# Where ScalarE's convolution products lie: raw weight buffers or scratch buffers

## The chip, the cores and the metric

The kernel runs on one core of a Trainium2 chip. The metric is the device time of one execution in microseconds (us), the median over runs. The engines are named as in the profile: PE is TensorE (matmuls, with PEld its weight loads), DVE is VectorE, ACT is ScalarE, POOL is GpSimd and SP is SyncE, whose queue issues the loads of the weights.

## The reference

It is a network of three blocks on 256 tokens of width 1024, all in float32: a first block (attention, a gated delta rule and a feed-forward net), then two layers of a second network, the first ("even") with a state-space scan and a convolution side by side, the second ("odd") with a gated recurrence; each of the two ends with a mixture of experts. The change is in the convolution of the even layer, a depthwise convolution of 31 taps over 1024 channels, done for 256 context tokens and, row by row of 64, for the 256 latent tokens:

```python
def dwconv(x, w, b):
    k = w.shape[0]
    y = lax.conv_general_dilated(x, w[:, None, :].astype(x.dtype), window_strides=(1,),
                                 padding=[(k // 2, k // 2)], dimension_numbers=("NWC", "WIO", "NWC"),
                                 feature_group_count=x.shape[-1])
    return y + b.astype(y.dtype)

def conformer_conv(v, gate, dw_w, dw_b, ln_g, ln_b, rows):
    u = v * jax.nn.sigmoid(gate)
    b, n, ch = u.shape
    if rows is not None:
        u = u.reshape(b * rows, GRID_W, ch)
    u = dwconv(u, dw_w, dw_b).reshape(b, n, ch)
    return jax.nn.silu(layernorm(u, ln_g, ln_b))
```

`v` and `gate` are columns of a projection of the tokens by the weight `ab_w_in` (1024 wide input).

## The kernel before, in words

Matmuls are made with each float32 operand split into a high and a low part, so that one product is three matmuls (L313 to L315: high by high, low by high, high by low). A weight comes through `load_split` (L277): SyncE loads a piece of 128x1024 floats into a buffer of tag `raw` (L284), ScalarE casts it to the high part `wh` (L287), and VectorE, or GpSimd for every third piece, subtracts to make the low part `wl` (L292). There are six `raw` buffers and three each of `wh` and `wl`. A buffer of a tag is handed to the next tile of that tag when its last reader is done. The order of instructions on each engine, and which buffer a tile gets, are settled by a scheduler before the program runs; on the chip each engine follows its queue.

The projection for the convolution is made in channel blocks of 128, two at a time (`proj_fm`, L317): for each pair first the gates (`g_cons`, L1108: a sigmoid on ScalarE into `cfg`), then the values (`v_cons`, L1119). One such projection of two blocks takes two pieces of the weight, for input rows 0 to 511 and 512 to 1023; both blocks use both pieces. After these eight projections come the state-space inputs (`bc_block`, `xs_block`, with their own convolution of 5 taps, `conv5`, L1206), again two pieces for two blocks.

The eight channel blocks of the long convolution are done in three ways:

- blocks 0, 2 and 4 on VectorE: 30 taps of two spans each, one multiply-add a span (L1165), into the accumulator `cf`;
- blocks 1 and 3 on GpSimd: ScalarE multiplies the whole input `us` by one tap (L1151) into half of a product tile `cfp`, and GpSimd adds its two spans to the accumulator (L1153). Two products share a tile of 128x1024 floats. This is 30 products, 15 tiles and 60 additions a block;
- blocks 5, 6 and 7 on TensorE: the input goes into a padded tile `up` (cleared by GpSimd at L1128, written by VectorE at L1130 and L1132), DMAs of SyncE spread it into `cr` (L1174), and 64 matmuls against diagonal weights `dg` make the sums (L1190).

The work of the first two kinds is not issued where it is written. `conv_v` yields small steps, which lie in a list for VectorE and one for ScalarE; `tick` (L989) takes some of them after other instructions: two from ScalarE's list after each cast of a weight piece, three from VectorE's after each subtraction, five after a product `us`. With `issue_after` a step is queued behind that instruction on its engine:

```python
TICKS = {"w": 3, "u": 5, "c5": 2, "E": 2, "z": 3, "aw": 2, "aE": 1}
CONV_POOL = (1, 3)
CONV_PE = (5, 6, 7)

ins = nc.scalar.activation(hi, raw, AF.Copy)
self.tick(ins, "aw", "a")
```

The scratch tag `t4` has three buffers of 1024 floats (`POOLS = dict(raw=6, raw2=2, wh=3, act=13, tmp=5, t4=3, ps=(3, 2, 2, 1))`, `t4` at L220). In this layer it holds the squares for the norms (`sq`), the scan's sums `ac2` (L1055, from here to the last of the masks of the scan, L1297), the three padded inputs `up`, half of the masks `E` (L1290) and later the centred tokens `cft`.

Of the kernel before, what the change touches and what calls it, by code (L numbers as in the profile page):

```python
# [7 lines left out]
F32 = mybir.dt.float32  # L8
# [10 lines left out]
P = 128  # L19
# [891 lines left out]
class Net(Net1):  # L911
# [99 lines left out]
    def even_mixer(self):  # L1011
# [123 lines left out]
        def conv_v(b, g):  # L1135

            acc = cf[b // 4][:, b % 4, :]
            w = lambda j: C("cf_dw_w_2", b * 32 + j)
            rows = lambda t: t[:, 256:].rearrange("p (r w) -> p r w", r=4)
            pool = b in CONV_POOL  # L1140
            if pool:
                yield lambda: nc.scalar.activation(acc, g, AF.Identity, scale=w(15), bias=C("cf_dw_b_2", b))
            else:
                yield lambda: nc.vector.tensor_scalar(acc, g, w(15), C("cf_dw_b_2", b), op0=ALU.mult, op1=ALU.add)
            pr = None

            def product(j, n):
                nonlocal pr
                if n % 2 == 0:
                    pr = self.wp.tile([P, 2, 512], F32, tag="raw", name="cfp", bufs=self.nraw)  # L1150
                nc.scalar.activation(pr[:, n % 2], g, AF.Copy, scale=w(j))  # L1151
                for a, s in spans(j, pr[:, n % 2]):
                    nc.gpsimd.tensor_tensor(a, a, s, ALU.add)  # L1153

            def spans(j, g):
                d = j - 15
                lo, hi = max(0, -d), max(0, d)
                return ((acc[:, lo:256 - hi], g[:, lo + d:256 - hi + d]),
                        (rows(acc)[:, :, lo:64 - hi], rows(g)[:, :, lo + d:64 - hi + d]))
            for n, j in enumerate([*range(15), *range(16, 31)]):  # L1160
                if pool:
                    yield lambda n=n, j=j: product(j, n)
                    continue
                for a, s in spans(j, g):
                    yield lambda a=a, s=s, j=j: nc.vector.scalar_tensor_tensor(a, s, w(j), a, op0=ALU.mult, op1=ALU.add)  # L1165
# [1416 lines left out]
```

## Time and profile before

| what | value |
|---|---|
| time, median of 3 runs | 2175.76 us (2174.41 to 2177.12) |
| profiled execution, its own time | 2166.01 us |
| its span, first to last instruction | 2163.9 us |
| mean granted clock of TensorE | 0.971 |
| busy share of the span: PE, DVE, ACT, POOL | 92%, 52%, 39%, 30% |
| products `cfp` (ACT, L1151) | 60, from 753.8 to 966.7 us |
| raw weight loads of `ab_w_in` (SP, L284) | 40, from 681.3 to 978.3 us |

All times of instructions are from the start of the span of that one profiled execution. Idle time of an engine stands in square brackets in a timeline, with what ended it.

### The profile page before, as it was taken

To read this page: it belongs to the slowest core of one execution; us is meant where nothing else is said; L and a number is where in the kernel's file an instruction comes from. 1 tells how busy PE (TensorE), PEld (TensorE's weight loads), DVE (VectorE), ACT (ScalarE), POOL (GpSimd) and SP (SyncE) were. 2 spreads that over 40 slices of the span, in tenths; PEclk is the share of its full clock that TensorE was granted. 3 is DMA by queue.
4 is the path that set the end of the run, shared out by engine and by line. 5 is a ranking of instruction groups with operands and counts; after the bars stand their busy time and mean duration, and the time that the engine had idled before them with its cause. 6 is when DMAs were issued, how large, how long until landed. Compare 5 with 4: busy or idle time off the path is not lost. (4 is left out here: it accounts for less than half of the span.)

```text
span 2163.9 us, 30084 instructions
## 1 busy us (share of the span) xinstructions
PE 2000.4 (92%) x11456; PEld 1451.1 (67%) x11456; DVE 1116.7 (52%) x1992; ACT 853.6 (39%) x1394; POOL 648.8 (30%) x515
## 2 busy tenths in 40 slices
PE   7999999989998889988889999998999999899996
PEld 6899877779976666766768746663487666634342
DVE  5755553554435754877686623331625556633332
ACT  5553455454334444654444132320335555411111
POOL 1413322224332255556655122121312223101110
PEclk9999999999999999989999999999999999999998
DMA  7534556667775126221124799998645224999993
GB/s 236 154 108 138 156 182 200 214 194 239 225 241 161 30 68 158 69 68 59 31 91 143 255 365 350 356 368 325 229 136 186 89 96 154 327 343 396 395 335 137
DMA packets 282844, 433.12 MB, mean 200 GB/s; under 512 B 33722, under 2 KB 159290, under 8 KB 282432
## 3 DMA queue, kind: packets, MB, share of 16 engines
q1 hardware_dynamic: 261696, 407.17, 56.0%
q10 hardware_dynamic: 16528, 10.12, 1.7%
q0 software_dynamic: 4464, 13.79, 1.7%
q8 instruction: 93, 1.52, 0.3%
q14 instruction: 63, 0.52, 0.1%
HBM read 420.17 MB, written 9.54 MB: 199 GB/s over the span
## 5 line engine op out<-in xcount | busy, mean ns | idle before, releaser
L287 ACT ACTIVATE wh<-raw 128x1024 fp32r<-128x1024 f32 x288 | 303.1, 1057 | 374.7 <-PE mm L314 146.3
L292 DVE TENSOR_TENSOR wl<-raw,wh 128x1024 fp32r<-128x1024 f32 x196 | 260.6, 1332 | 296.4 <-ACT wh L287 293.5
L292 POOL TENSOR_TENSOR wl<-raw,wh 128x1024 fp32r<-128x1024 f32 x92 | 222.0, 2413 | 578.8 <-ACT wh L287 539.6
L2054 PE MATMUL mm<-we,xs 128*64 128x512 f32 x832 | 195.6, 614 | 13.2 <-DVEq L2215 9.0
L2054 PEld LDWEIGHTS mm<-we,xs 128*64 128x64 f32 x832 | 61.7, 141 | 135.9 <-issue 117.7
L1165 DVE SCALAR_TENSOR_TENSOR cf<-us,cols,cf 128x200 f32<-128x200 f32 (+14 forms) x180 | 121.9, 724 | 0.1
L2070 DVE TENSOR_TENSOR hh<-mm,hh 128x512 f32<-128x512 f32 x19 | 13.1, 692 | 204.2 <-PE mm L2054 136.8
L1153 POOL TENSOR_TENSOR cf<-cf,cfp 128x241 f32<-128x241 f32 (+14 forms) x120 | 93.7, 811 | 70.9 <-ACT cfp L1151 70.9
L2069 ACT ACTIVATE hh<-mm 128x512 f32<-128x512 f32 x22 | 13.1, 598 | 223.9 <-PE mm L2054 162.4
L313 PE MATMUL mm<-fh,wh 128*128 128x256 f32 x352 | 101.1, 287 | 0.0
L315 PE MATMUL mm<-fh,wl 128*128 128x256 f32 x352 | 100.0, 284 | 0.9 <-POOL wl L292 0.9
L314 PE MATMUL mm<-fl,wh 128*128 128x256 f32 x352 | 99.7, 283 | 0.0
L313 PE MATMUL mm<-uh,wh 128*128 128x256 f32 x320 | 96.6, 302 | 0.0
L315 PE MATMUL mm<-uh,wl 128*128 128x256 f32 x320 | 91.8, 287 | 1.8 <-DVE wl L292 1.5
L314 PE MATMUL mm<-ul,wh 128*128 128x256 f32 x320 | 92.9, 290 | 0.0
L2040 POOL TENSOR_TENSOR h<-h,yz 128x512 f32<-128x512 f32 x16 | 25.0, 1565 | 221.9 <-DVE yz L2039 221.9
L315 PE MATMUL mm<-ev0h,wl 128*128 128x512 f32 (+1 forms) x168 | 66.6, 397 | 8.4 <-DVE wl L292 8.4
L313 PEld LDWEIGHTS mm<-fh,wh 128*128 128x128 f32 x352 | 67.5, 192 | 5.4 <-issue 5.4
L313 PE MATMUL mm<-ev0h,wh 128*128 128x512 f32 (+1 forms) x168 | 68.0, 406 | 0.7 <-ACT wh L287 0.7
L315 PEld LDWEIGHTS mm<-fh,wl 128*128 128x128 f32 x352 | 67.5, 192 | 1.4 <-POOL wl L292 1.3
L313 PE MATMUL mm<-ev1h,wh 128*128 128x512 f32 (+1 forms) x168 | 65.8, 392 | 2.5 <-ACT wh L287 2.5
L2054 PE MATMUL mm<-we,hT 128*64 128x512 f32 x208 | 60.9, 600 | 7.5 <-ACT hT L1934 7.5
(968 smaller groups left out, 5228.8 us busy)
## 6 DMA issues: line engine op xcount, KB each, us to landing
mraw<-in_mod_w SPq DMA_DIRECT2D x96, 512.0 KB
we<-in_moe_w_gate SPq DMA_DIRECT2D x37, 1024.0 KB
raw<-in_w_in SPq DMA_DIRECT2D x72, 512.0 KB
we<-in_moe_w_down SPq DMA_DIRECT2D x35, 1024.0 KB
we<-in_moe_w_up SPq DMA_DIRECT2D x32, 1024.0 KB
we<-in_moe_w_up SPq DMA_DIRECT2D x52, 512.0 KB
we<-in_moe_w_down SPq DMA_DIRECT2D x46, 512.0 KB
we<-in_moe_w_gate SPq DMA_DIRECT2D x42, 512.0 KB
```

The costliest lines, as they stand in the source:

```text
L287: ins = nc.scalar.activation(hi, raw, AF.Copy)
L292: ins = eng.tensor_tensor(lo, raw, hi.bitcast(F32), ALU.subtract)
L313: mm(out, lh, rh, start=start, stop=False)
L314: mm(out, lh, rl, start=False, stop=False)
L315: return mm(out, ll, rh, start=False, stop=stop)
L1153: nc.gpsimd.tensor_tensor(a, a, s, ALU.add)
L1165: yield lambda a=a, s=s, j=j: nc.vector.scalar_tensor_tensor(a, s, w(j), a, op0=ALU.mult, op1=ALU.add)
L2040: (nc.gpsimd if d else nc.vector).tensor_tensor(x[:, t, ds], x[:, t, ds], z, ALU.add)
L2054: nc.tensor.matmul(out[r], x[0][:, k, r], w, start=start, stop=stop)
L2069: nc.scalar.activation(hh, pg[2 * i], AF.Silu)
L2070: nc.vector.tensor_tensor(hh, pg[2 * i + 1], hh, ALU.mult)
```

## The change

Product tiles take a buffer of tag `t4` in place of one of tag `raw`. Shape, size and type of the tile are the same (two halves of 512 floats), and all instructions stay.

```diff
@@ -1147,7 +1147,7 @@
             def product(j, n):
                 nonlocal pr
                 if n % 2 == 0:
-                    pr = self.wp.tile([P, 2, 512], F32, tag="raw", name="cfp", bufs=self.nraw)
+                    pr = self.t4([P, 2, 512], name="cfp")
                 nc.scalar.activation(pr[:, n % 2], g, AF.Copy, scale=w(j))
                 for a, s in spans(j, pr[:, n % 2]):
                     nc.gpsimd.tensor_tensor(a, a, s, ALU.add)
```

```python
def t4(self, shape=None, dt=F32, name="t4"):
    return self.tp.tile(shape or [P, 1024], dt, tag="t4", name=name, bufs=self.n4)
```

## Rows read from the trace of the kernel before

**Rows 1.** The page, busy us, share of the span and instructions of each engine

```profile
PE 2000.4 (92%) x11456; PEld 1451.1 (67%) x11456; DVE 1116.7 (52%) x1992; ACT 853.6 (39%) x1394; POOL 648.8 (30%) x515
```

**Rows 2.** Instructions on tile `cfp`: ns min/median/max, first and last start

```profile
L1151 ACT ACTIVATE cfp<-us,cols x60: 701/710/754, 753.8 to 966.7; 128x512 f32<-128x512 f32 x60
```

**Rows 3.** Windows: stretch, length, busy us (instructions) PE, PEld, DVE, ACT, POOL, clock, DMA

```profile
750.00:860.00 110.00, 98.06 (x629) 75.01 (x632) 62.64 (x86) 48.93 (x68) 62.22 (x71) 0.97 0.41 108
```

**Rows 4.** Timeline of PE: start, us, what, count, idle time before and its releaser

```profile
763.84 0.50 PE L313 MATMUL mm<-ev0h,wh 128*128 128x512 f32 x1 [0.70 <-ACT wh L287]
...
784.48 0.80 PE L315 MATMUL mm<-ev0h,wl 128*128 128x512 f32 x1 [8.10 <-DVE wl L292]
...
823.65 0.51 PE L313 MATMUL mm<-ev1h,wh 128*128 128x512 f32 x1 [2.54 <-ACT wh L287]
...
824.91 0.51 PE L315 MATMUL mm<-ev1h,wl 128*128 128x512 f32 x1 [0.53 <-DVE wl L292]
```

**Rows 5.** Windows behind the second of these gaps

```profile
784.50:788.50 4.00, 4.00 (x10) 3.13 (x11) 3.41 (x7) 0.00 (x0) 0.00 (x0) 0.50 0.61 148
788.50:800.00 11.50, 11.50 (x52) 9.54 (x51) 2.40 (x4) 5.60 (x9) 3.19 (x6) 1.00 0.26 87
```

**Rows 6.** Timeline of DVE, 773 to 787 us

```profile
773.02 0.69 DVE L1122 TENSOR_TENSOR us<-mm,cfg 128x512 f32<-128x512 f32 x1 [6.00 <-PE mm L315]
773.63 3.66 DVE L1165 SCALAR_TENSOR_TENSOR cf<-us,cols,cf 128x224 f32<-128x224 f32 x5
...
777.81 5.48 DVE L1165 SCALAR_TENSOR_TENSOR cf<-us,cols,cf 128x251 f32<-128x251 f32 x5
783.21 1.21 DVE L292 TENSOR_TENSOR wl<-raw,wh 128x1024 fp32r<-128x1024 f32 x1
784.35 1.24 DVE L1165 SCALAR_TENSOR_TENSOR cf<-us,cols,cf 128x244 f32<-128x244 f32 x3
785.51 1.21 DVE L292 TENSOR_TENSOR wl<-raw,wh 128x1024 fp32r<-128x1024 f32 x1
```

**Rows 7.** Timeline of ACT: casts near 770 and 822 us, an evacuation at 872

```profile
767.57 1.05 ACT L287 ACTIVATE wh<-raw 128x1024 fp32r<-128x1024 f32 x1
...
822.54 1.06 ACT L287 ACTIVATE wh<-raw 128x1024 fp32r<-128x1024 f32 x1 [8.95 <-DMA raw<-in_ab_w_in]
...
871.97 0.78 ACT L1209 ACTIVATE c<-mm,cols 128x512 f32<-128x512 f32 x1 [4.55 <-PE mm L315]
```

**Rows 8.** Waits of SP, 680 to 860 us: total us, times, longest

```profile
SPq L284 <- ACT cfp L1151: 21.0, 3, 10.2
...
SPq L284 <- POOL cf L1153: 11.8, 6, 4.3
```

**Rows 9.** Timeline of DVE at 728 us and of SP, 728 to 757.2 us

```profile
728.07 1.23 DVE L292 TENSOR_TENSOR wl<-raw,wh 128x1024 fp32r<-128x1024 f32 x1 [0.56 <-ACT wh L287]
...
734.40 22.93 SPq L284 DMA_DIRECT2D raw<-in_ab_w_in  x2
```

**Rows 10.** The page, costliest groups: the additions, busy us, mean ns, idle before

```profile
L1153 POOL TENSOR_TENSOR cf<-cf,cfp 128x241 f32<-128x241 f32 (+14 forms) x120 | 93.7, 811 | 70.9 <-ACT cfp L1151 70.9
```

**Rows 11.** Tile `up` and the timelines of POOL and DVE: the pads

```profile
L1128 POOL MEMSET up<- x3: 612/612/616, 734.3 to 820.2; 128x620 f32 x3
...
820.18 0.62 POOL L1128 MEMSET up<- 128x620 f32 x1 [4.97 <-DMA cr<-up]
...
827.62 0.42 DVE L1130 TENSOR_TENSOR up<-mm,cfg 128x256 f32<-128x256 f32 x1 [0.30 <-PE mm L315]
```

**Rows 12.** Timeline of POOL: additions and a subtraction, 798 to 852 us

```profile
798.02 4.96 POOL L1153 TENSOR_TENSOR cf<-cf,cfp 128x254 f32<-128x254 f32 x8 [3.77 <-ACT cfp L1151]
...
808.17 7.04 POOL L1153 TENSOR_TENSOR cf<-cf,cfp 128x253 f32<-128x253 f32 x8
...
824.35 3.50 POOL L1153 TENSOR_TENSOR cf<-cf,cfp 128x249 f32<-128x249 f32 x4 [3.55 <-ACT cfp L1151]
...
849.37 2.40 POOL L292 TENSOR_TENSOR wl<-raw,wh 128x1024 fp32r<-128x1024 f32 x1 [3.32 <-ACT wh L287]
```

## Prediction

> **What bounds the kernel now.** I read the page first. TensorE is busy for 92% of the span and no other engine for more than 52% [rows 1], so a change pays where it closes a gap of TensorE, or costs where it opens one. The products that the change moves, 60 on ScalarE, start from 753.8 to 966.7 us [rows 2], with 120 additions behind them on GpSimd [rows 10], so I asked for the stages there. From 750 to 860 us TensorE is idle for 110.00 - 98.06 = 11.94 us [rows 3]. The timeline of TensorE shows four gaps that make up nearly all of it: 0.70, 8.10, 2.54 and 0.53 us, 11.87 in all [rows 4]. The reader should see that each of them ends with a weight part (`wh` from ScalarE, `wl` from VectorE) that came too late, and none with an addition or a product of the convolution. The long gap also costs after its end: for 4.00 us ten matmuls run at a granted clock of 0.50, that is 1.2 GHz, and then 52 take 11.50 us at 1.00 [rows 5]: 0.400 us against 0.221, so 10 x 0.179 = 1.8 us more.
>
> Why were the parts late? Two views answer. In the timeline of VectorE, the subtraction that ends the 8.10 us gap starts at 783.21, though its cast ran on ScalarE from 767.57 and took 1.05 [rows 6, 7]. VectorE sat idle for 6.00 us before 773.02, waiting for a matmul at an instruction that stands ahead of the subtraction in its queue, and then did this one and 10 taps (3.66 + 5.48 us) first [rows 6]. So the order was fixed when the program was scheduled, and the scheduler did not expect that weight so soon. The second view is SyncE's waits. Of the loads of raw weights, three waits are put down to a product on ScalarE (21.0 us) and six to additions on GpSimd (11.8 us) [rows 8]: the loads queue for buffers that products hold. And a buffer is held before its product exists. A subtraction frees a raw buffer at 728.07 + 1.23 = 729.30, but the two loads in the stretch are issued at 734.40 and (the last 0.37 us of 22.93) 756.96 [rows 9], while the first product starts only at 753.8 [rows 2]. I read this as buffers of a tag being given out in program order: what is free at 729 is kept for products that stand ahead of the next load.
>
> **The change part by part.** It removes 30 tiles (60 products, two in a tile) from the six raw buffers and adds them to the three scratch buffers. Operations, shapes, engines and DMAs stay: 60 products of 0.710 us and 120 additions of 93.7 / 120 = 0.78 us [rows 2, 10]. So their own cost is zero, and all of the sum is in who gets a buffer when.
>
> *Loads.* All six raw buffers go to weights. One product tile stands in program order between any two weight tiles, so without them the load that was issued at 756.96 takes a buffer some three tiles earlier, near 729, about 27 us sooner. This should move casts and subtractions ahead in the order of their engines. The gap of 0.70 us ends on a cast of such a weight: it goes. The gap of 2.54 us ends on a cast that waited 8.95 us for a load [rows 4, 7]: it goes, with the 0.53 behind it. Together 3.77 us.
>
> *The gap of 8.10 us.* If the late subtraction (1.21 us) and its three taps (1.24 us) go ahead of the matmul wait, into the 6.00 us idle, the next weight half's subtraction, now from 785.51, starts at 783.21 and ends at 784.42 [rows 6]. TensorE then has work of the first half alone: 24 matmuls for both blocks at 0.227 us (5.4 us, to 781.8) or 12 for one block (2.7 us, to 779.1). What is left of the gap is 2.6 or 5.3 us, the gain 5.5 or 2.8. Below that lies nothing, if VectorE's order stays; above it 8.10, if the second half too gets ahead. I take 4.1, the middle of the two. Of the 1.8 us at half clock I take 0.9, between all and none.
>
> *Scratch.* One of the three scratch buffers holds the scan's sums (`ac2`) until the last of the masked exponentials far behind this stage; two are left, which the padded inputs `up` of blocks 5 to 7 share. Handed out in program order, `up` of block 5 stands behind product tile 7 (two products follow each weight part's cast, from block 2's first part on), that of block 6 behind tile 11. In the trace the first two pads are cleared at 734.3, at once when they can be, and the third waited 4.97 us on GpSimd for a pad's DMA before 820.18 [rows 11]: these three uses already fill the scratch. After the change the pad of block 5 is cleared near 800, after the first additions from 798.02, some 20 us before that landing; block 6's is cleared after the first two additions from 824.35, near 826.7 with its 0.61 us, and is needed at 827.62 [rows 11, 12]. So these are just hidden; if not, VectorE's next subtraction stands behind it. While a pad holds one buffer, products have one, and ScalarE must wait for additions. Four products that before ran between 805 and 810 use two tiles; the eight additions from 808.17 took 7.04 us [rows 12], so a tile is held 3.5 us longer than now. What ScalarE's wait costs the path is at least nothing (it idles 8.95 us a little later [rows 7]) and at most the 3.5 us of one hold; I take 2.0, a little over the middle.
>
> It is here that a rule of the Trainium skill speaks against the change: TensorE: Matmul & The Clock Gate, section on the 16 sub-arrays (engine queue depths), says that ScalarE's and VectorE's queues are strictly first in, first out. The 6.00 us at 773.02 with a ready subtraction behind agrees. By that rule alone a held product stops each cast queued behind it, and the gain would be the smaller by 3.5 instead of 2.0.
>
> *Sum.* 3.77 + 4.1 + 0.9 - 2.0 = 6.8 us, say 7. The profiled execution took 2166.01 us (span 2163.9); it would take 2159, and the median of the runs, 2175.76 and so 9.75 above it, 2169. The most that the loads can give is 11.87 + 1.8 = 13.7 us.
>
> **The rivals.** *The order stays (no change).* If the scheduler still puts the taps ahead of the subtraction, 8.10 and 1.8 us stay. Left are 3.77 us less a hold of 0 to 3.5 on ScalarE: from 3.8 to 0.3 us faster, 2172 to 2175. For it: taps stand before that weight in program order. Against: VectorE's 6.00 us of idle [rows 6], which an earlier load could fill.
>
> *The pads take the scratch first (slower).* If a buffer goes to whoever is ready, the pads of blocks 5 and 6 keep both from 734.3, as now [rows 11], and the first product waits until a pad's DMA lands, 820.2. Block 1's 60 additions then take 60 x 0.78 = 47 us, with three subtractions of 2.4 us between them until about 874. The subtraction now at 849.37 [rows 12] would come behind them and end near 876. TensorE wants that weight 12 matmuls (2.7 us) before the evacuation at 871.97 [rows 7], at 869, or at 862 when the loads have given their 7 us. It loses up to 14 us, net 7: 2183. It decides against the change once the subtraction ends more than 7 us after 862. For it: the memsets at 734.3. Against it: the raw buffer that no load took at 729.30 [rows 9]. In this case the additions would also be gone from the stretch before 783, where a tap takes 1.1 us (five in 5.48) instead of 0.41 (three in 1.24) [rows 6].
>
> *The change doesn't do what it says:* the freed raw buffers are not used earlier, since casts wait for TensorE to free `wh` buffers, not for loads; one of the two casts that end a gap did wait for a load, which speaks against it [rows 7]. Then nothing moves by more than the holds, 2176 to 2180.
>
> **How the numbers follow.** A measurement here tells 0.2%, 4.35 us, from no change. The forecast gets 0.50, of which 0.03 stays within that bound; the order that stays 0.28 (0.24 within, 0.04 slower, by several holds); the pads first 0.18 (0.16 slower, 0.02 within); no effect 0.04 (0.03 within, 0.01 slower). So faster 0.47, same 0.32, slower 0.21. The forecast's own range is 2162 to 2172. The range reaches down to 2161, where all the gaps close, and up to 2184, where the pads' case stands with its price; outside is left a hold longer than 14 us, or a gain in later stages that I don't see.
>
> **What would show it.** Right: loads of raw weights no longer wait for products or additions in SyncE's waits; the first product still starts near 754; the gap near 776 is under 6 us and that near 821 gone; ScalarE or its products show waits for GpSimd's additions near 800 to 815. The pads are cleared near 800, 826 and 831. Wrong: both pads cleared at 734 and the first product near 820; a new gap of TensorE at a GpSimd subtraction between 850 and 880; or VectorE waiting for a memset of `up`. The prediction fails as a whole if a gap that I call gone is replaced by one of its size later, between 860 and 1000.

## The result and the profile after

| | before | after |
|---|---|---|
| time, median of 4 runs | 2175.09 us (2173.32 to 2177.12) | 2148.93 us (2145.31 to 2153.08) |
| profiled execution, span | 2166.01, 2163.9 | 2151.28, 2149.5 |
| mean granted clock of TensorE | 0.971 | 0.974 |

The ratio is 0.9878, 95% interval 0.9859 to 0.9897: 26 us faster, where 7 had been forecast, and below the range that was given (2161 to 2184). The direction was right; the size was not.

I read the change by stages. Four events on ScalarE cut both traces at the same places: the second gate `cfg`, the first x block's evacuation (`c` from `mm`), the last `c<-c`, the first z block's evacuation, the last one. First before, then after; the columns are those of [rows 3]. Stage 1 begins 5.5 us later in the trace of after; over the 17 profiles of this document it begins anywhere from 746.6 to 755.7, at 753.9 and 755.7 in the two of the changed kernel, so clock times of two traces compare only from there.

```profile
748.40:845.70 97.30, 85.36 (x458) 66.68 (x458) 51.49 (x72) 40.23 (x56) 55.44 (x65) 0.96 0.41 105
845.70:958.50 112.80, 105.57 (x674) 82.72 (x673) 93.36 (x131) 69.00 (x111) 58.90 (x63) 0.98 0.26 75
958.50:986.50 28.00, 20.69 (x82) 15.86 (x83) 17.58 (x29) 13.94 (x34) 17.14 (x20) 0.76 0.31 94
986.50:1089.80 103.30, 90.66 (x445) 73.20 (x444) 69.50 (x118) 47.28 (x123) 64.34 (x67) 0.93 0.13 34
```

```profile
753.90:836.40 82.50, 82.50 (x461) 65.89 (x460) 53.21 (x72) 40.90 (x56) 57.75 (x65) 1.00 0.51 136
836.40:950.10 113.70, 108.95 (x695) 84.93 (x694) 96.39 (x134) 71.99 (x117) 63.23 (x66) 1.00 0.26 75
950.10:968.80 18.70, 14.27 (x62) 10.72 (x61) 11.28 (x25) 12.37 (x34) 12.39 (x16) 0.91 0.00 1
968.80:1072.20 103.40, 90.14 (x445) 73.34 (x444) 69.69 (x121) 45.10 (x120) 65.74 (x69) 0.93 0.13 34
```

I call them stages 1 to 4. They change by -14.8, +0.9, -9.3 and +0.1 us, -23.1 in all. TensorE's idle time (length less busy, summed) falls from 39.12 to 22.44 us, and its busy time from 302.28 to 295.86 for the same matmuls; the granted clock is higher in stages 1 to 3. Stage 1 has no idle time left. In stage 3 TensorE does 62 matmuls where it did 82; 21 more stand in stage 2 (695 against 674), 20 of them with weights (L313 to L315): z matmuls that now come before the scan and fill gaps there. What lies between 23.1 and the 26 of the medians is within the interval (22 to 31 us). The two profiled executions differ by 14.7 us only, as that of before was short outside of the four stages (2163.9 - 341.4 = 1822.5 us, after 1831.2; a second profiled execution of after 1836.0).

The queue of VectorE in stage 1 answers to [rows 6]:

```profile
770.09 2.73 DVE L292 TENSOR_TENSOR wl<-raw,wh 128x1024 fp32r<-128x1024 f32 x1 [2.31 <-ACT wh L287]
774.66 0.69 DVE L1122 TENSOR_TENSOR us<-mm,cfg 128x512 f32<-128x512 f32 x1 [1.83 <-PE mm L315]
775.27 3.43 DVE L1165 SCALAR_TENSOR_TENSOR cf<-us,cols,cf 128x224 f32<-128x224 f32 x5
778.62 1.21 DVE L292 TENSOR_TENSOR wl<-raw,wh 128x1024 fp32r<-128x1024 f32 x1
780.10 0.69 DVE L1122 TENSOR_TENSOR us<-mm,cfg 128x512 f32<-128x512 f32 x1 [0.27 <-PE mm L315]
```

The two subtractions that ran at 783.21 and 785.51, behind both products `us` and all their taps, now stand one ahead of each `us`, in time in which VectorE had waited. The loads, in the timeline of SyncE from 732 to 760 us and then in its waits from 680 to 860 us, answer to [rows 8, 9]:

```profile
732.75 7.83 SPq L284 DMA_DIRECT2D raw<-in_ab_w_in  x3
```

```profile
SPq L284 <- DVE wl L292: 75.9, 13, 21.2
SPq L284 <- POOL wl L292: 62.9, 9, 13.4
```

Three loads go out by 740.6, where before one did at 734.40 and the next at 756.96, and in these waits no load waits for a product or an addition. Counted from the first load of `ab_w_in`, the three are the ninth to the eleventh; before, the ninth went out at 756.96 and the eleventh at 771.51. The other side, ScalarE's products (tile `cfp`; [rows 2]), and then ScalarE's waits in stage 1:

```profile
L1151 ACT ACTIVATE cfp<-us,cols x60: 704/711/742, 759.6 to 957.8; 128x512 f32<-128x512 f32 x60
```

```profile
ACT cfp L1151 <- POOL cf L1153: 18.1, 7, 3.6
ACT wh L287 <- PE mm L314: 11.9, 6, 4.8
ACT cfp L1151 <- DMA cr<-up: 5.8, 2, 4.2
```

Products do wait for a scratch buffer now, in stage 1 18.1 us in seven waits for additions and 5.8 in two for a pad, yet the stage shows no gap. The second line says why they could: casts behind them waited 11.9 us for matmuls, which are the last readers of `wh` buffers, so ScalarE was ahead of TensorE there. The pads [rows 11] are cleared in their turn among the products:

```profile
792.24 0.62 POOL L1128 MEMSET up<- 128x620 f32 x1
813.57 0.62 POOL L1128 MEMSET up<- 128x620 f32 x1
819.03 0.62 POOL L1128 MEMSET up<- 128x620 f32 x1
```

### The profile page after: what moved, and what is told of

Same layout as the page of the kernel before. It is cut to its first block, busy times and chain, and to the rows that moved or that the text cites. A ratio compares the mean times of both kernels' runs of the same rounds, so it can differ in the third digit from the quotient of the medians.

```text
span 2149.5 us, 30094 instructions
## 1 busy us (share of the span) xinstructions
PE 1998.3 (93%) x11456; PEld 1452.1 (68%) x11456; DVE 1113.5 (52%) x1992; ACT 853.8 (40%) x1394; POOL 651.5 (30%) x515
## 5 line engine op out<-in xcount | busy, mean ns | idle before, releaser
L313 PE MATMUL mm<-fh,wh 128*128 128x256 f32 x352 | 100.9, 287 | 0.0
L315 PE MATMUL mm<-fh,wl 128*128 128x256 f32 x352 | 99.8, 284 | 0.9 <-POOL wl L292 0.9
L313 PE MATMUL mm<-uh,wh 128*128 128x256 f32 x320 | 97.0, 303 | 0.0
L315 PE MATMUL mm<-uh,wl 128*128 128x256 f32 x320 | 92.2, 288 | 1.6 <-DVE wl L292 1.5
L313 PEld LDWEIGHTS mm<-fh,wh 128*128 128x128 f32 x352 | 67.4, 191 | 5.4 <-issue 5.4
L315 PEld LDWEIGHTS mm<-fh,wl 128*128 128x128 f32 x352 | 67.4, 192 | 1.4 <-POOL wl L292 1.3
L314 PEld LDWEIGHTS mm<-fl,wh 128*128 128x128 f32 x352 | 67.5, 192 | 0.0
L932 PE MATMUL mx<-mraw,cs 128*32 128x256 f32 x768 | 59.7, 395 | 7.5 <-DMA mraw<-in_mod_w 7.5
L313 PE MATMUL mm<-ev0h,wh 128*128 128x512 f32 (+1 forms) x168 | 66.5, 397 | 0.0
```

What stands on the lines that cost most here:

```text
L313: mm(out, lh, rh, start=start, stop=False)
L314: mm(out, lh, rl, start=False, stop=False)
L315: return mm(out, ll, rh, start=False, stop=stop)
L932: self.together(lambda g: nc.tensor.matmul(ps[32 * g:32 * g + 32, d:d + 256], self.cs[:, k, :], w[:, g, :], start=(k == 0), stop=(k == 7)), 4)
```

## The experiments

All of them in one table: the ratio to the kernel before on the same chip, its 95% interval, and the lengths of the four stages by the same events in the profiled execution. "Sum" is theirs. The runs: blk1 and blk3 change one block's products; own2r4, own3r3 and own1r5 give the products two, three and one buffers of their own and leave the weights four, three and five; t4raw5 is the change with five raw buffers; t1prod puts each product into a small scratch tile, raw1each into a raw buffer; tickend and flush edit the order of the program before, tickflush does both, t4flush is flush on the change; r2prod and b1t4b3t1 use other tags; after_again is the change once more.

| run | median us | ratio | 1 | 2 | 3 | 4 | sum |
|---|---|---|---|---|---|---|---|
| before | | 1 | 97.3 | 112.8 | 28.0 | 103.3 | 341.4 |
| after | 2148.93 | 0.9878 (0.9859 to 0.9897) | 82.5 | 113.7 | 18.7 | 103.4 | 318.3 |
| blk1 | 2161.08 | 0.9928 (0.9905 to 0.9952) | 82.5 | 112.0 | 27.6 | 104.4 | 326.5 |
| blk3 | 2163.90 | 0.9942 (0.9917 to 0.9967) | 96.9 | 113.7 | 17.9 | 100.7 | 329.0 |
| own2r4 | 2158.55 | 0.9923 (0.9895 to 0.9951) | 82.2 | 113.6 | 16.5 | 102.2 | 314.6 |
| own3r3 | 2190.44 | 1.0068 (1.0041 to 1.0094) | 82.2 | 113.7 | 16.5 | 102.2 | 314.6 |
| own1r5 | 2157.80 | 0.9930 (0.9904 to 0.9956) | 86.8 | 114.9 | 17.9 | 102.9 | 322.5 |
| t4raw5 | 2156.85 | 0.9904 (0.9877 to 0.9930) | 83.3 | 113.4 | 18.5 | 104.3 | 319.5 |
| t1prod | 2153.67 | 0.9904 (0.9877 to 0.9930) | 82.9 | 118.6 | 21.0 | 95.9 | 318.4 |
| raw1each | 2175.62 | 1.0013 (0.9996 to 1.0030) | 97.8 | 111.8 | 29.0 | 100.6 | 339.2 |
| tickend | 2159.57 | 0.9917 (0.9895 to 0.9939) | 82.6 | 112.0 | 27.8 | 100.5 | 323.0 |
| flush | 2164.24 | 0.9948 (0.9924 to 0.9973) | 97.7 | 115.6 | 15.0 | 99.9 | 328.2 |
| tickflush | 2148.44 | 0.9870 (0.9845 to 0.9895) | 82.5 | 115.4 | 15.0 | 103.7 | 316.6 |
| t4flush | 2147.85 | 0.9868 (0.9833 to 0.9904) | 82.6 | 115.8 | 13.3 | 103.8 | 315.4 |
| r2prod | 2152.31 | 0.9892 (0.9870 to 0.9914) | 82.3 | 114.3 | 24.2 | 93.9 | 314.7 |
| b1t4b3t1 | 2152.41 | 0.9900 (0.9873 to 0.9927) | 82.9 | 117.8 | 21.5 | 97.2 | 319.5 |
| after_again | 2152.56 | 0.9893 (0.9872 to 0.9915) | 82.5 | 113.7 | 18.7 | 103.5 | 318.4 |

**One block's products alone.** My first theory was supply: the weights get all six raw buffers. The rivals: pace (products that wait for one of two buffers spread the work of ScalarE and GpSimd), and an order reshuffled by chance.

```diff
-pr = self.wp.tile([P, 2, 512], F32, tag="raw", name="cfp", bufs=self.nraw)
+pr = self.t4([P, 2, 512], name="cfp") if b == 1 else self.wp.tile([P, 2, 512], F32, tag="raw", ...)
```

> Only the products of block 1 lie in scratch; those of block 3 stay in the buffers of raw weights. The whole change shortened two stages of the profiled execution: the one from the first gate of the convolution to the first x block (97.30 to 82.50 us, 14.8 less) and the one from the last x block to the first z block (28.00 to 18.70 us, 9.3 less). Theory A, supply (weights that get all six raw buffers are loaded sooner, and their casts and subtractions come sooner in the order of their engines): block 1's products run in the first stage, so that stage takes 82 to 85 us; in the late stage block 3's products hold raw buffers as before, so it keeps 26 to 29 us. Time 2158 to 2163 us. Theory B, pace (the gain comes from products that wait for one of two scratch buffers, which spreads ScalarE's and GpSimd's work): the same for the first stage, but block 3's products are not paced and the stage in between and the late one are as before: 2158 to 2163 us too; this run tells the places apart, not A from B. Theory C, a reshuffled order (any change of the program's order here gives some new schedule, and the gain has nothing to do with a stage's own buffers): the stages don't follow the blocks; the late stage may be short, or the first one long.

The complement has `b == 3`:

> Only the products of block 3 lie in scratch; those of block 1 stay in the buffers of raw weights: the complement of the run with block 1 alone. Theory A, supply: the first stage keeps 95 to 99 us, since block 1's products hold raw buffers in it; the late stage takes 18 to 21 us. Time 2163 to 2168 us, and the two complements add up to the gain of the whole, 26 us, within 5 us. Theory B, pace: the same split. Theory C, reshuffled order: the two parts don't add up, or the late stage stays at 28 us.

First block 1 alone, then block 3 alone, stages 1 and 3:

```profile
753.60:836.00 82.40, 82.40 (x459) 65.81 (x458) 53.17 (x72) 40.88 (x55) 58.34 (x67) 1.00 0.48 122
...
948.10:975.60 27.50, 20.22 (x81) 15.51 (x82) 17.53 (x29) 13.94 (x33) 17.11 (x20) 0.76 0.32 96
```

```profile
746.60:843.50 96.90, 85.52 (x460) 66.76 (x459) 51.57 (x72) 40.27 (x56) 54.99 (x65) 0.95 0.41 105
...
957.10:975.00 17.90, 14.58 (x65) 11.15 (x64) 11.37 (x24) 12.40 (x35) 12.39 (x16) 0.90 0.00 1
```

Each block's products cost in one place, and the parts add up: 15.7 us by the ratio of the one (0.72% of 2178.03) and 12.6 by that of the other, 28 against 26 for the whole. A reshuffle by chance is out.

**How many buffers.** The products get buffers of their own, taken from the six, and one run takes a raw buffer from the changed kernel.

```diff
-pr = self.wp.tile([P, 2, 512], F32, tag="raw", name="cfp", bufs=self.nraw)
-POOLS = dict(raw=6, ...)
+pr = self.wp.tile([P, 2, 512], F32, tag="cfp", name="cfp", bufs=2)
+POOLS = dict(raw=4, ...)
```

> The products lie in two buffers of their own, and the raw weights get four buffers instead of six: the memory is that of the kernel before, split by hand. Nothing else may be done with the products' buffers, and no pad shares them. Theory A, supply: the weights have fewer buffers than with the change (four, not six) at all times, also in the rest of the kernel where there are no products, so most of the gain is lost: the first stage takes 90 to 100 us, the late one 22 to 30, and other stages lose; time 2165 to 2200 us. Theory B, pace: the products wait for two buffers as with the change (and are not held by pads), so the gain in both stages stays: 82 to 85 and 18 to 21 us, time 2147 to 2155 us, unless other stages without products lose by the four buffers, which the table of stages would show.

> The kernel after, with five raw buffers instead of six: products in scratch as with the change. Theory A, supply: the weights have one buffer less, still more than before the change in the stages where two to three product tiles were alive; from a gain of 26 us a part is lost, 3 to 12 us: time 2152 to 2161 us, with gaps of TensorE that end on a cast or a subtraction again. Theory B, pace: the products are paced as with the change, time 2147 to 2153 us.

With four raw buffers for the weights stages 1 and 3 are as short as with six, so supply by number fell here, and pace looked better, though 2158.55 us lies between the times that the two had foretold. I formed another theory, decoupling (a load must not wait for a buffer that a product leaves late), and split the six 3 and 3, then 1 and 5:

> The split of the six buffers by hand once more, three for the products and three for the raw weights. With two and four the first stage took 82.24 us and the late one 16.52, as short as with the change, so that the number of the weights' buffers is not what the gain comes from there. Theory A2, decoupling (a load of a weight gets the buffer of a tile that stands some places earlier in the same ring; when that is a product tile, the load waits for additions on GpSimd that are late for reasons of their own; in a ring of weights alone it waits for a subtraction only): three weights in flight still don't wait for products; the first stage takes 82 to 88 us, the late one 16 to 20, and the waits of the loads in both stages name subtractions alone; the rest of the kernel pays for three buffers. Time 2155 to 2185 us, the loss outside of the stages. Theory A, supply by the number of buffers: three are clearly too few, the first stage takes 95 us or more. Theory B, pace: with three buffers the products wait less than with two (18.1 us of ScalarE's waits with the change, 6.5 with two of their own); if the pace gave the gain, the first stage would go back towards 97 us.

> One buffer for the products and five for the raw weights. Each pair of products must wait until the four additions of the pair before it are done, so ScalarE is held most. Theory A2, decoupling: the loads name subtractions alone, the late stage stays at 16 to 20 us and the first at 82 to 87 us; ScalarE waits for additions longer than with two (over 18 us in the first stage), which may cost a few us where a cast stands behind a held product. Time 2148 to 2162 us. Theory B, pace: the more the products wait the better: the first stage 80 to 82 us, time at or under 2149 us.

Three buffers give the same 82.2 and 16.5 us, so number is out for these stages, and pace too: these products wait least, and one buffer, where they wait most, makes stage 1 longer again. The time with three, 2190.44 us, is above what had been expected (2155 to 2185). ScalarE's waits in stage 1 with one product buffer, and its window, which has a gap again:

```profile
ACT cfp L1151 <- POOL cf L1153: 37.9, 14, 4.5
```

```profile
747.60:834.40 86.80, 85.04 (x461) 67.14 (x459) 51.89 (x72) 40.87 (x56) 57.02 (x65) 0.98 0.47 125
```

Its trace shows the path from a held product to that gap: a product held 2.67 us until 762.41, behind it a gate and, at 764.95, a cast, GpSimd's subtraction of that weight at 766.07, and the end of TensorE's gap of 1.70 us at 768.48.

What the fewer raw buffers cost lies elsewhere: with three, 2188.3 - 314.6 = 1873.7 us lie outside of the stages, against 1822.5 in the profile of before and at most 1839.4 in any other run's (own2r4, with four). There the mixture of experts loads its weights into the same tag. The wait of these loads over the whole span, before and with three:

```profile
SPq L1587 <- PE mm L2054: 66.6, 26, 12.3
```

```profile
SPq L1587 <- PE mm L2054: 162.9, 34, 15.6
```

The run with five raw buffers is inconclusive. Its time, 2156.85 us, lies in the range of supply (2152 to 2161) and above that of pace, but stage 1 has no gap of TensorE as supply had foretold, and its interval overlaps that of the changed kernel.

**Small tiles, and the ring doubled.** One product in a tile, from the small scratch, or from the raw buffers as before:

```diff
-if n % 2 == 0:
-    pr = self.wp.tile([P, 2, 512], F32, tag="raw", name="cfp", bufs=self.nraw)
-nc.scalar.activation(pr[:, n % 2], g, AF.Copy, scale=w(j))
+pr = self.t1(name="cfp")      # or: self.wp.tile([P, 512], F32, tag="raw", name="cfp", bufs=self.nraw)
+nc.scalar.activation(pr, g, AF.Copy, scale=w(j))
```

> Each product lies in a buffer of its own of 512 floats from the ring of the small scratch tiles (five buffers, shared with the gates and the convolution sums), and not in the raw weights' or the large scratch buffers; the raw weights have all six. Theory A2, decoupling: the weights are as free as with the change, and the pads of the other convolution blocks no longer share buffers with products: both stages are as short as with the change or by up to 2 us shorter, time 2143 to 2151 us, unless the gates wait for products, which would show as a wait of TensorE in the first stage. Theory B, pace: products of one each in a ring of five wait less than with the change, and the first stage would be longer than 85 us: time 2155 to 2170 us.

> The kernel before, but each product takes a raw buffer of its own, of which it fills half, so that 60 product tiles instead of 30 stand in the ring of raw weights: the suspected cost doubled. Theory A2, decoupling: more loads take over a buffer of a product, so the loads wait more for products and additions (before: 39.4 us in the waits of the loads in the first stage, products and additions together); the first stage takes 100 to 115 us and the late one 28 to 36. Time 2180 to 2200 us. Theory B, pace: the products wait as little as before, the stages stay within 2 us of 97 and 28, time 2172 to 2180 us.

The small tiles again make stage 1 short, 82.9 us; stage 3 (21.0, with 23 matmuls that the change has in stage 4) and the time (2153.67) are longer than decoupling had foretold. The doubled ring was a miss for decoupling: nothing got slower, though the loads of stage 1 waited longer for products and additions. Pace had foretold that, but the run with three buffers rules it out. The waits of SyncE there, then the gap in the timeline of TensorE:

```profile
SPq L284 <- ACT cfp L1150: 47.6, 5, 26.7
SPq L284 <- DVE cf L1164: 21.8, 2, 14.8
SPq L284 <- POOL cf L1152: 12.9, 6, 3.2
```

```profile
786.62 0.80 PE L315 MATMUL mm<-ev0h,wl 128*128 128x512 f32 x1 [8.15 <-DVE wl L292]
```

The first and third line are 60.5 us, where the same two are 17.8 + 9.1 = 26.9 us in stage 1 of before (the 39.4 of the expectation is not what that view gives); the load that before issues 8.5 us behind the second gate is issued 17.0 behind it, and the gap is still 8.15 against 8.10 [rows 4]. So the gap doesn't follow the time at which the load gets its buffer on the chip. What stays the same in both kernels is the program's order: products are written ahead of the same loads, and VectorE's queue in stage 1 has the same order, instruction for instruction.

**The order alone.** Theory three, place: the scheduler hands buffers out in the order in which the program is written. A product that is written ahead of a load must get its buffer first, and it is written to follow something that comes late; the load, with its cast and subtraction, is then reckoned late, and VectorE's queue is ordered by that. This can be tested with the buffers of before: only write the products behind both loads of a projection (its two pieces of weight), not each pair behind its own cast. The edit writes them behind both casts and subtractions too, so it moves the instructions together with their tiles.

```diff
-            self.tick(ins, "aw", "a")
+            casts.append(ins)
...
+        for ins in casts:
+            self.tick(ins, "aw", "a")
```

> The buffers of the kernel before (products in the six raw buffers), but the products that follow the casts of a piece of weights are written in the program behind all loads of that piece, not one pair behind each cast; each pair is still issued after its cast. So in the ring of raw buffers a piece's weight tiles stand next to each other, ahead of the product tiles. Theory A3, place (buffers are handed out in the program's order, so a product tile that is written ahead of a load must get its buffer first; the load, and in the scheduler's reckoning its cast and subtraction, comes that much later, and the order of ScalarE's and VectorE's queues is fixed by that reckoning): the loads of a piece come ahead of its products, most of the gain is there without any other buffer: first stage 82 to 90 us, late one 18 to 24, time 2150 to 2162 us. Theory A2, release (the loads wait for buffers that products leave late, because additions on GpSimd are late): the product tiles are in the same ring and leave it as late as before, so a load of the next piece waits as before: first stage 94 to 100 us, late one 25 to 30, time 2168 to 2182 us.

Its stages 1 and 3:

```profile
750.40:833.00 82.60, 82.60 (x460) 66.04 (x459) 53.12 (x72) 40.59 (x55) 59.48 (x65) 1.00 0.49 127
...
945.00:972.80 27.80, 20.31 (x82) 15.78 (x83) 19.34 (x29) 13.60 (x34) 17.89 (x20) 0.75 0.31 95
```

All of stage 1's gain, with the products in the ring of six as before, and with loads that still wait for additions (11.5 us in six waits) and once for a product (4.7 us). The ninth load goes out at 758.44, no earlier than before, and the gap is gone all the same. Release, which is decoupling under another name, is refuted there, place holds: the runs with buffers of their own keep the written order and change the ring, this one keeps the ring and changes the written order, and both have the gain.

The kept traces show what the length of stage 1 goes with. VectorE's 73 instructions from the first `us` to the last `up` stand in one of three orders. In before, blk3, raw1each and flush (96.9 to 97.8 us) the third and the fourth subtraction stand behind the fourth `us`. In the eleven profiles in which at least block 1's products lie outside of the raw buffers (82.2 to 83.3 us, with one product buffer 86.8) the third stands ahead of the third `us` and the fourth ahead of the fourth. In the two with this edit (82.6 and 82.5 us) both stand between the third and the fourth `us`.

Stage 3 did not move, against what place had foretold (18 to 24 us): its products are not written behind casts but, one by one, behind the scan's exponentials (`aE` in `TICKS`). The waits of the loads from 930 to 1000 us in the kernel before have one of them:

```profile
SPq L284 <- ACT cfp L1151: 15.7, 1, 15.7
```

So the leftover products were written ahead of the scan:

```diff
+        for f in self.later["a"]:
+            f()
+        self.later["a"] = []
         steps = [(g, c) for g in range(4) for c in range(4)]
```

> The buffers and the order of the kernel before, but the products that are still left when the scan begins are written ahead of the scan's steps instead of one behind each group of the scan's exponentials. Theory A3, place (a product tied to an exponential of the scan stands in the ring ahead of a load of z weights, so that load waits for the scan's progress, while the scan has no other work of TensorE to fill its waits): the late stage falls from 28.03 to 18 to 22 us, the first stays at 97 us; the last 103 us stage within 4 us. Time 2164 to 2171 us. Rival, number (z's loads need more buffers than the ring leaves while products are in it): the products stay in the ring, so the late stage stays at 26 to 30 us, time 2171 to 2180 us.

> Both edits of the program's order, with all products in the six raw buffers as before: a piece's products behind its loads, and the scan's leftovers ahead of the scan. Theory A3, place: first stage 82 to 84 us, late one 18 to 22, time 2146 to 2156 us, so that the change's gain is there without its buffers. Rival, number: as the run with the first edit alone, 82.64 and 27.79 us, time 2157 to 2163 us.

> The changed kernel with the scan's leftovers written ahead of the scan. Theory A3, place: the z loads are not behind products any more, so there is nothing to gain: late stage 17 to 20 us, time 2147 to 2155 us, the same as the changed kernel. Rival (the products behind the scan's exponentials cost by their time on ScalarE and GpSimd, not by their place in the ring): the late stage falls by a further 2 to 4 us, to 15 to 17 us, as in the runs with two buffers of their own (16.52), time 2143 to 2148 us.

The last eight loads of `ab_w_in`, in the timeline of SyncE before and with the second edit alone, then windows of the second edit alone (stages 1 to 3) and of both edits (all four):

```profile
932.43 46.24 SPq L284 DMA_DIRECT2D raw<-in_ab_w_in  x8
```

```profile
936.38 21.38 SPq L284 DMA_DIRECT2D raw<-in_ab_w_in  x8
```

```profile
750.60:848.40 97.80, 85.79 (x460) 66.98 (x460) 51.57 (x72) 40.31 (x57) 54.84 (x65) 0.95 0.40 103
848.40:964.00 115.60, 110.40 (x695) 86.38 (x693) 99.34 (x135) 73.55 (x117) 68.96 (x71) 0.99 0.33 97
964.00:979.00 15.00, 13.71 (x61) 10.62 (x62) 11.68 (x23) 10.98 (x33) 8.47 (x9) 0.89 0.00 1
```

```profile
748.40:830.80 82.40, 82.40 (x459) 65.84 (x459) 53.12 (x72) 40.61 (x55) 59.84 (x65) 1.00 0.49 131
830.80:946.30 115.50, 109.12 (x695) 85.19 (x694) 99.22 (x136) 73.62 (x117) 66.83 (x70) 1.00 0.31 91
946.30:961.20 14.90, 12.31 (x60) 9.31 (x61) 11.90 (x23) 10.88 (x32) 8.40 (x9) 1.00 0.00 1
961.20:1065.00 103.80, 90.94 (x446) 73.28 (x445) 71.04 (x121) 45.21 (x120) 65.89 (x69) 0.93 0.13 34
```

Before, the last of these loads go out inside stage 3 (the end is 978.7, the stage 958.5 to 986.5); with the edit all are out by 957.8, ahead of it (964.0). One load still waits 11.8 us for a product there, so here too the wait by itself isn't the price. Stage 3 falls below what was expected, to 15.0 us, and the 21 matmuls more are in stage 2 (695). Part of it is a move: stage 2 is 2.8 us longer with the products that were brought forward. The two edits of order together give 0.9870 with the products in the raw buffers, the ratio of the change.

On the changed kernel the second edit leaves the time within the interval, and 2147.85 us fits place and its rival. Stage 3 does not: 13.3 us, where place had foretold 17 to 20 and the rival, that the products behind the exponentials cost by their time, 15 to 17. Of its matmuls 22 moved into stage 4 (40 and 467, with the change 62 and 445); stages 2 and 3 together are 3.3 us shorter, 129.1 against 132.4. The rival can't be the main cause in stage 3 all the same. With buffers of their own, and still behind the exponentials, stages 2 and 3 take 130.1 us (two buffers) and 130.2 (three), as little as in the raw buffers with the edit (130.6, with both edits 130.4; before 140.8). What the 3.3 us are is open; the products share the scratch tag with half of the masks `E`, and no run takes that apart.

**For a faster kernel.** Two other places for the products:

```diff
+pr = self.raw2([P, 2, 512], "cfp")                        # r2prod, all products
+one = self.t1(name="cfp") if b == 3 else <half of a t4 tile>   # b1t4b3t1
```

> The products lie in the two buffers for 1024 floats that the kernel otherwise uses, in these stages, for the diagonal weights of the convolution blocks on TensorE; the raw weights have six, the pads have the scratch as before the change. The run with two buffers of their own and four raw had the four stages together in 314.6 us against 318.3 with the change and lost more than that elsewhere. Theory A3 or A2, products out of the ring: if the diagonal weights don't get in the way, the stages take 314 to 319 us, and the rest keeps six raw buffers: time 2141 to 2151 us, the fastest so far. Against it: the diagonal weights of a block are held until its matmuls on TensorE, so that products may wait for one buffer or for both; one buffer cost 4.6 us in the first stage (86.82 against 82.24): then 2150 to 2160 us.

> Block 1's products in the large scratch as with the change, those of block 3 one by one in the ring of small scratch tiles. With all products in small tiles the second stage took 118.60 us and the fourth 95.89 (with the change 113.68 and 103.45); the sum of the four was the same, 318.4 against 318.3. If these two differences come from block 3's products, which run from the second stage on, this kernel has both too and takes as long as the change, 2146 to 2152 us; if the longer second stage comes from block 1's and the shorter fourth from block 3's, 2141 to 2146 us.

> The changed kernel itself, beside the others on the same chip, to compare with: 2146 to 2152 us, ratio 0.986 to 0.990, stages of 82.5, 113.7, 18.7 and 103.4 us within 1 us, since the order is fixed in the program.

Neither is faster than the changed kernel beside them. In the two buffers of the diagonal weights the stages sum to 314.7 us, 3.7 less, and the median is the same 2152 us; 3 us in the stages are too little to be told in the time; that it would be the fastest was a miss. In the run with block 3 in small tiles, stage 2 is long and stage 4 short as in that with all: both come from block 3. None of the versions beats the changed kernel by what can be measured; the two edits of order match it.

## Why the prediction was wrong in size

- **The loads** (right). The loads no longer wait for products or additions, and go out earlier much as forecast: the ninth, for which near 729 instead of 756.96 had been named, at 732.75 us. The reading behind it, buffers given out in the program's order, is what the two edits of order confirm. The rival "the pads take the scratch first" is refuted by the pads at 792 to 819 us (forecast: 800 to 831) and products from 759.6, 5.7 us behind the start of the stage (before 5.4); "no effect" and "the order stays" by the ratio and by VectorE's queue.
- **Together 3.77 us** (right): the gaps of 0.70, 2.54 and 0.53 us are gone.
- **The gap of 8.10 us** (the first step that failed): "I take 4.1, the middle of the two". The upper end came true, "8.10, if the second half too gets ahead": both subtractions moved, to 770.09 ahead of the third `us` and to 778.62 ahead of the fourth. I had costed the first half's move and treated the second's as a bound; loads that come in order ahead of the products bring both halves sooner.
- **The half clock** ("of the 1.8 us I take 0.9"): the stretch at half clock is gone with the gap, so its whole 1.8 us count; the clock of stage 1 is 1.00, before 0.96. TensorE's busy time in the stage falls by more, 2.86 us, 85.36 to 82.50. The other 1.1 us are in no stretch at half clock, and what they are stays open.
- **Scratch** ("I take 2.0"): the holds are there, 18.1 + 5.8 us in stage 1, and cost TensorE nothing in it, so the term was 0; the casts waited for TensorE themselves. It is real with one buffer: 86.8 - 82.2 = 4.6 us against two or three of their own. So stage 1 gave 11.94 + 2.86 = 14.8 us for the 6.8 of the sum, a little over the 13.7 that I had named as the most. The Trainium skill, TensorE: Matmul & The Clock Gate, section on the 16 sub-arrays (engine queue depths), has ScalarE's queue strictly first in, first out. The trace with one buffer agrees: the cast at 764.95 ran behind the product that was held until 762.41.
- **Stage 3** (the second step that failed): the sum has no term there; I looked for gaps from 750 to 860 us only, and named "a gain in later stages that I don't see" just as something outside of the range. [Rows 2] had products up to 966.7 us, and the same question there, what the loads wait for from 930 us on, shows the 15.7 us wait for a product. The stage became 9.3 us shorter, 8.4 with what stage 2 gives back.

With 14.8 and 8.4 in the sum the forecast would have been 2175.8 - 23.2 = 2152.6. The range failed for the same reason: its low end, 2161, stood for all gaps of one stage. Shown by runs: the two places, that they add up, that either the ring or the written order of the products gives the whole gain in both, and that neither the number of the weights' buffers nor pace does. Shown by the traces: stage 1's length goes with the order of VectorE's queue in all 17 profiles, own1r5's short gap aside. Only argued: that the scheduler's reckoning of the load's time is what set that order; no run forced it by itself.

## What to carry to other kernels

A buffer of a shared tag is a place in a queue: where a scheduler hands buffers out in program order, a tile that is written ahead of a load can delay it, and with it the planned order of all that the load feeds. In these two stages three buffers without the products did for the weights what six with them did not. Look for it over the whole life of the tiles that move, not in the stage with the largest gap, and before spending memory try to write the loads first. Where a gap comes from the order of a queue, expect one of the orders with its whole price, not a value between them.

## What was not expected of the hardware

The subtraction of 128x1024 on VectorE took 2.73 us at 770.09 and 1.21 us at 778.62. What GpSimd did beside them, in its timeline of the changed kernel:

```profile
769.34 2.40 POOL L292 TENSOR_TENSOR wl<-raw,wh 128x1024 fp32r<-128x1024 f32 x1
771.71 6.34 POOL L1153 TENSOR_TENSOR cf<-cf,cfp 128x246 f32<-128x246 f32 x8
778.97 3.62 POOL L1153 TENSOR_TENSOR cf<-cf,cfp 128x250 f32<-128x250 f32 x4 [0.92 <-ACT cfp L1151]
```

The slow one started while a subtraction ran on GpSimd and ended 1.08 us behind it (769.34 + 2.40 = 771.74, 770.09 + 2.73 = 772.82), as if it had only begun then. All profiles together have 198 such subtractions on VectorE, which started during one on GpSimd. They took 1.21 to 2.76 us, and every one ended 1.08 to 1.17 us behind GpSimd's. With nothing on GpSimd one of this size took 1.16 to 1.23 us; beside additions there, 1.21 to 1.76. The 1.52 us more were covered here: VectorE waited 1.83 us for a matmul right behind it.

In stage 1 the granted clock was 0.99 or 1.00 in every run without a gap of TensorE, and 0.95 to 0.98 in those with one.
